# A gated DeltaNet trunk on one core: the causal mask moves from TensorE and the exponent to a clamp on ScalarE and a select on GpSimd

## The chip, the cores and the metric

The kernel runs on one core of a Trainium2 chip. The metric is the device time of one execution in microseconds (us), as the median over several runs. The engines are named as the profile names them: PE is TensorE (PEld its weight load), DVE is VectorE, ACT is ScalarE, POOL is GpSimd, and SP is SyncE, which here issues most DMAs. All arrays are float32.

## The reference

The reference is a decoder trunk of two layers over 512 tokens of width 1024: a gated DeltaNet mixer (16 value heads, 8 query and key heads, head dimension 128), a gated MLP with a short convolution, a sliding-window attention over shared keys and values, a second such MLP, and a final norm. The change lies in the mixer. Cut to what matters there (`gc` is the running sum of the log gates within a chunk, which only falls):

```python
diff = gc[..., :, None] - gc[..., None, :]
decay = jnp.where(tril, jnp.exp(jnp.where(tril, diff, 0.0)), 0.0)
m = jnp.where(strict, jnp.einsum('bnhcd,bnhsd->bnhcs', k_beta, k) * decay, 0.0)
t_mat = lax.linalg.triangular_solve(m + eye, eye, left_side=True, lower=True, unit_diagonal=True)
a_intra = jnp.einsum('bnhcd,bnhsd->bnhcs', q, k) * decay
def step(state, inp):
    w_i, u_i, qd_i, kd_i, a_i, gl_i = inp
    v_new = u_i - jnp.einsum('bhcd,bhde->bhce', w_i, state)
    o_i = (jnp.einsum('bhcd,bhde->bhce', qd_i, state)
           + jnp.einsum('bhcs,bhse->bhce', a_i, v_new))
    state = state * gl_i[..., None, None] + jnp.einsum('bhcd,bhce->bhde', kd_i, v_new)
```

So two matrices are needed per head and chunk: `m`, for the triangular solve, and `a_intra`, the attention weights within the chunk. Both are products of keys or queries with the same decay, and both are zero on one side of the diagonal.

## The kernel before

Everything is kept transposed: 128 channels on the partitions, 512 tokens along the free dimension, and chunks of 128 tokens. A dense product is a *pass* of 24 matmuls (L162, L163, L164 in `mm3`): eight blocks of 128 input channels, each as high half of the weights times high half of the input, high times low, and low times high. The halves of the weights come from a staged load: ACT casts a tile of 128x1024 to the high half `whi` (L132) and DVE subtracts to get the low half `wlo` (L133). There are three buffers of each, two stages, three PSUM banks `d` for the passes, and two banks `g` which the gate products share with the transposes.

The mixer's 16 heads are worked in four groups of four. Each group goes through jobs that are named by letters:

- K projects a key (conv and Silu, `conv_silu`, L277 to L281); B makes the products of the keys of a chunk with themselves (L433, copied out by ACT at L434) and the norms (a square root on ACT, L446).
- P (`key_products`, L458 to L486) makes the decay and the matrix for the solve. Per head a matmul (L464) spreads the running gates `gr` of that head over a bank of 128x512. A second matmul (L465), identity times a mask of 0 and -2^100, adds the mask to the same bank. Four Exp on ACT (L475), one per chunk of 128 tokens with the negated gate of the partition as bias, leave the decay in the row `dt`. DVE scales it (L477) and multiplies it with the key products (L479), and SP writes the diagonal blocks to DRAM for the solve.
- I solves the 32x32 blocks on DVE (L555, L561); L joins them to 128x128 (`levels`, short products on PE with copies by ACT: pz at L587 and L588, p6s at L608).
- Q projects and R normalises queries, A (`query_products`, L504 to L512) multiplies keys and queries (L508) and then the scaled decay (L511, DVE) into the tile `at`. T turns the keys, V projects values (scaled copies vt on ACT, L538).
- C is one step of the scan over the chunks: products with the state (L635), the solve's inverse (L651), a copy us by ACT (L653), products with the keys and with `at` (L659), squares on ACT (L682).
- z and g are the output gates (Silu sz on ACT, L705) and the gated norms of a finished group (L720 on ACT).

The table ORDER gives the jobs of each group in a row and the scheduler gives them priorities by their place, with an offset by letter (SHIFT); the dense passes of the jobs K, Q, V and z are thus spread between the short products. The order on each engine is then decided by a scheduler that simulates the program when it is built: it takes the ready instruction of highest priority, so an instruction that becomes ready later or lasts longer changes the order behind it. What has been put into an engine's row is executed in that order: an engine waits at the first instruction that is not ready. A function that ACT has not loaded needs an ACT_TABLE_LOAD ahead of it.

The job order of the first group, and the offsets:

```python
"K1 B P0 P1 I0 I1 V0 I2 I3 T1 Q0 Q1 A1 A0 V1 R T0 V2 V3 L0 L1 C0 C1 C2 C3",
...
SHIFT = {"R": 6, "B": -28, "g": -40, "K": -1, "N": 7, "C": -2, "P": -3}
```

The output gates and norms of one group run beside the next, and behind the mixer come the output projection, MLP, attention and MLP (from about 430 us on), which the change does not touch.

Of the kernel before, what the change touches and what calls it, by code (L numbers as in the profile page):

```python
# [8 lines left out]
F32 = mybir.dt.float32  # L9
F32R = mybir.dt.float32r  # L10
BF16 = mybir.dt.bfloat16
AF = mybir.ActivationFunctionType
ALU = mybir.AluOpType
# [4 lines left out]
P = 128  # L18
T = 512
NC = T // P  # L20
# [21 lines left out]
def kernel(  # L42
# [27 lines left out]
    V, S, G, PE, SP = nc.vector, nc.scalar, nc.gpsimd, nc.tensor, nc.sync  # L70
# [1 line left out]


    cp = ctx.enter_context(tc.tile_pool(name="const", bufs=1))
    cp.tile([P, 40], F32, name="gap_x")
    dp = ctx.enter_context(tc.tile_pool(name="scratch", bufs=1, space=DRAM))

    cnt = [0]
# [1 line left out]
    def nm(s):  # L80
        cnt[0] += 1
        return f"{s}_{cnt[0]}"
# [24 lines left out]
    def row(tag, dt=F32, n=T):  # L107
        return main.tile([P, n], dt, tag=tag, bufs=ROWS[tag], name=nm(tag))

    def pair(tag, dt=F32):  # L110
        return main.tile([P, 2, T], dt, tag=tag, bufs=PAIRS[tag], name=nm(tag))

    def bank(tag):
        return psum.tile([P, T], F32, tag=tag, bufs=BANKS[tag], name=nm(tag))

    def const(shape, dt=F32, s="c"):
        return cp.tile(list(shape), dt, name=nm(s))
# [64 lines left out]
    def together(makes, *after):  # L182
        first = None
        for make in makes:
            if first is None:
                first = make()
                for a in after:
                    behind(first, a)
            else:
                with tc.high_priority(JUMP):  # L190
                    behind(make(), first)
# [16 lines left out]
    for i in range(2):  # L208
        cs = slice(HQK * P + i * P, HQK * P + (i + 1) * P)
# [3 lines left out]

    ident = const([P, P], s="ident")
    make_identity(nc, ident[:])
    identr = const([P, P], F32R, s="identr")
    S.copy(identr[:], ident[:])
    ones = const([P, P], s="ones")
    V.memset(ones[:], 1.0)
    epsc = const([P, 1], s="eps")  # L220
# [42 lines left out]
    for k in range(KD):  # L263
        ps = bank("g") if k % 2 else bank("s")
        for c in range(NC):
            PE.transpose(ps[:, c * P : (c + 1) * P], xs[c][:, k * P : (k + 1) * P], ident[:])
        h, l = row("xh", F32R), row("xl", F32R)
# [65 lines left out]
    for c in range(NC):  # L333
        cs = slice(c * P, (c + 1) * P)
        V.tensor_tensor_scan(R[32:48, cs], ones[32:48, 0:P], sp_r[32:48, cs], 0.0, op0=ALU.mult, op1=ALU.add)
    for c in range(NC):
        cs = slice(c * P, (c + 1) * P)
# [4 lines left out]
    gr = row("gr", F32R)[:, :]  # L342
# [8 lines left out]
    G.affine_select(sk[:], sk[:], pattern=[[-1, 16]], compare_op=ALU.not_equal, fill=1.0, base=-32, channel_multiplier=1)  # L351
    skr = const([P, 16], F32R, s="skr")
    S.copy(skr[:], sk[:])
    mneg = row("acc", n=P)
    G.memset(mneg[:], 0.0)
    G.affine_select(
        mneg[:],
        mneg[:],
        pattern=[[1, P]],
        compare_op=ALU.is_ge,  # L360
        fill=-(2.0**100),
        base=0,
        channel_multiplier=-1,
    )
    mnegr = const([P, P], F32R, s="mnegr")
    S.copy(mnegr[:], mneg[:])

    gtp = bank("g")
    turned_gates = [
        PE.transpose(gtp[:, c * 80 : c * 80 + 80], R[0:80, c * P : (c + 1) * P], ident[0:80, 0:80])  # L370
# [5 lines left out]
    def hc(ap):  # L376
        return ap.rearrange("p c h -> p h c")

    beta_t, gc_t, gd_t = hc(gt[:, :, 0:16]), hc(gt[:, :, 32:48]), hc(gt[:, :, 64:80])
    ngc = const([P, 16, NC], s="ngc")  # L380
    V.tensor_scalar(ngc[:], gc_t, -1.0, None, op0=ALU.mult)
    egc = const([P, 16, NC], s="egc")
    S.activation(egc[:], gc_t, AF.Exp)
    negegc = const([P, 16, NC], s="negegc")
# [73 lines left out]
    def key_products(g, i):  # L458
        st[g]["nt", i] = pair("nt")
        for j in range(2):  # L460
            hh = 2 * i + j
            h = 4 * g + hh
            ps = bank("g")
            PE.matmul(ps[:], skr[:, h : h + 1].to_broadcast([P, P]), gr, start=True, stop=False)  # L464
            PE.matmul(  # L465
                ps[:].rearrange("p (c t) -> p c t", c=NC),
                identr[:],
                mnegr[:].unsqueeze(1).to_broadcast([P, NC, P]),
                start=False,
                stop=True,  # L470
            )
            dt = row("dt")
            for c in range(NC):
                cs = slice(c * P, (c + 1) * P)
                S.activation(dt[:, cs], ps[:, cs], AF.Exp, bias=ngc[:, h, c : c + 1])  # L475
            d3 = dt[:].rearrange("p (c t) -> p c t", c=NC)
            V.tensor_tensor(d3, d3, brk[:, h, :].unsqueeze(2).to_broadcast([P, NC, P]), op=ALU.mult)  # L477
            nt = st[g]["nt", i][:, j, :]
            V.tensor_tensor(nt, st[g]["kk"][:, i, :], dt[:], op=ALU.mult)  # L479
            for b in range(4):  # L480
                bs = slice(32 * b, 32 * b + 32)
                SP.dma_start(
                    nd[g, hh, :, b, :, :].rearrange("n s c -> s n c"),
                    nt[bs, :].rearrange("p (n c) -> p n c", n=NC)[:, :, bs],
                )
            st[g]["dt", hh] = dt  # L486
# [17 lines left out]
    def query_products(g, i):  # L504
        pq = bank("g")
        k, q = st[g]["k"][:, i, :], st[g]["q"][:, i, :]
        cut = [slice(c * P, (c + 1) * P) for c in range(NC)]
        together([lambda cs=cs: PE.matmul(pq[:, cs], k[:, cs], q[:, cs], start=True, stop=True) for cs in cut])  # L508
        at = pair("at")
        for j in range(2):  # L510
            V.tensor_tensor(at[:, j, :], pq[:], st[g]["dt", 2 * i + j][:], op=ALU.mult)  # L511
            st[g]["at", 2 * i + j] = at[:, j, :]  # L512

    def key_tokens(g, i):
# [220 lines left out]
    def bias_rows():  # L735
# [14 lines left out]
    JOBS = {  # L750
        "K": key_proj,
        "P": key_products,
        "I": solve,
        "Q": query_proj,
        "A": query_products,
        "T": key_tokens,
        "V": value_proj,
# [7 lines left out]
    base = tc.cur_priority  # L765
    pos = 0
    for i, line in enumerate(ORDER):
        for word in line.split():
            a, n = word[0], [int(d) for d in word[1:]]
# [77 lines left out]
    for m2 in range(KD // 2):  # L847
        sts = [load_stage(a_w_out[0], 1024 * u, 8, 256 * m2) for u in range(2)]
        for j in range(2):
            m = 2 * m2 + j  # L850
            ps = bank("d")
# [592 lines left out]
```

## Time and profile before

| | |
|---|---|
| median of 3 runs | 1417.68 us (1416.81 to 1419.02) |
| span of the profiled execution | 1412.6 us |
| PE, DVE, ACT, POOL busy | 1384.7, 1108.1, 748.1, 15.6 us |
| mean granted clock of PE, by stage | 1.00 throughout |
| gate products L464 and L465, first to last | 49.5 to 320 us |
| table loads on ACT | 36 |

The three runs' times are those of whole executions; the profiled one is known by its span, which lies 5.1 us under their median. "Busy" adds the time that an engine was executing; matmuls overlap, so the distance from start to start tells more of what one costs than its own length. An idle time is put down to the instruction that released the engine. In an answer of the trace `L132 ACT CAST whi<-stage 128x1024 ... x2` is line 132, engine, operation, the tile written and the tile read, shape, and how many such instructions were taken together.

### The profile page before, as it was taken

The page shows a single profiled execution, that of the slowest core. Times are in us where ns is not written, and L with a number is a line of the kernel's source. Part 1 is how long each engine was busy: PE and PEld are TensorE (multiplying, and loading weights), DVE is VectorE, ACT ScalarE, POOL GpSimd, SP SyncE. Part 2 cuts the span into 40 slices and gives each one's busy share as a digit, 9 for nine tenths or more (in the row PEclk, how much of TensorE's full clock was granted, in tenths as well). Part 3 has the DMA queues.
Part 4 walks back from the last instruction along what each step waited for, and adds up shares of the span by engine and source line. Part 5 has one row for each costly group of instructions (what it writes and reads, how often), then busy time and mean ns, then how long its engine had stood idle before and what let it go on. Part 6 is the DMA issues. An engine that isn't in the chain of part 4 may idle for free.

```text
span 1412.6 us, 21751 instructions
## 1 busy us (share of the span) xinstructions
PE 1384.7 (98%) x8370; PEld 1167.1 (83%) x8370; DVE 1108.1 (78%) x2070; ACT 748.1 (53%) x1470; POOL 15.6 (1%) x37
## 2 busy tenths in 40 slices
PE   7999999999999999999999999999999999999998
PEld 5787888878877888888988889777788888988897
DVE  4996896978856438879878889788668888878996
ACT  7764566656658225444344446567544444444543
POOL 1000000000100000000000000000000000000000
PEclk9999999999999999999999999999999999999999
DMA  5333254172465323221443223322132231432222
GB/s 161 92 103 115 79 175 126 61 231 84 140 225 159 119 90 112 90 90 46 135 150 119 75 79 109 109 71 76 61 112 90 90 101 49 146 106 82 92 75 75
DMA packets 162299, 151.80 MB, mean 107 GB/s; under 512 B 24148, under 2 KB 150677, under 8 KB 162197
## 3 DMA queue, kind: packets, MB, share of 16 engines
q1 hardware_dynamic: 159938, 150.22, 33.2%
q8 instruction: 66, 1.08, 0.3%
q10 hardware_dynamic: 2259, 0.20, 0.1%
q14 instruction: 36, 0.29, 0.1%
HBM read 133.60 MB, written 15.75 MB: 106 GB/s over the span
## 4 chain that ended last, share of the span: by engine, by line
PE 87%; DVE 6%; DMA 2%; ACT 2%; issue 1%; SPq 0%; DVEq 0%; ACTq 0%
PE d L162 20%; PE d L163 20%; PE d L164 20%; PE g L198 2%; DVE wlo L133 2%; PE d L1054 1%; PE d L1207 1%; PE d L1211 1%; PE d L1209 1%; PE d L1052 1%; PE d L1053 1%; PE s L1054 1%; PE s L1052 1%; PE s L1053 1%; PE s L659 1%
## 5 line engine op out<-in xcount | busy, mean ns | idle before, releaser
L162 PE MATMUL d<-xh,whi 128*128 128x512 f32 x1128 | 444.2, 394 | 0.2
L163 PE MATMUL d<-xl,whi 128*128 128x512 f32 x1128 | 444.0, 394 | 0.0
L164 PE MATMUL d<-xh,wlo 128*128 128x512 f32 x1128 | 441.9, 393 | 0.3 <-DVE wlo L156 0.3
L132 ACT CAST whi<-stage 128x1024 fp32r<-128x1024 f32 (+2 forms) x234 | 227.4, 976 | 247.7 <-PE d L163 165.1
L133 DVE TENSOR_TENSOR wlo<-stage,whi 128x1024 fp32r<-128x1024 f32 (+2 forms) x234 | 263.4, 1128 | 70.4 <-ACT whi L132 69.6
L162 PEld LDWEIGHTS d<-xh,whi 128*128 128x128 f32 x1128 | 211.7, 188 | 44.9 <-ACT xh L172 0.5
L164 PEld LDWEIGHTS d<-xh,wlo 128*128 128x128 f32 x1128 | 211.6, 188 | 44.6 <-DVE wlo L156 0.7
L163 PEld LDWEIGHTS d<-xl,whi 128*128 128x128 f32 x1128 | 211.7, 188 | 43.2 <-issue 0.5
L280 DVE SCALAR_TENSOR_TENSOR acc<-d,cwc,acc 128x511 f32<-128x511 f32 (+2 forms) x96 | 70.7, 739 | 8.7 <-ACT acc L277 7.9
L913 DVE TENSOR_TENSOR sz<-d,p6s 128x512 f32<-128x512 f32 x59 | 40.6, 688 | 42.9 <-PE d L164 40.7
L935 ACT ACTIVATE dt<-dt 128x512 f32<-128x512 f32 x44 | 27.8, 631 | 78.3 <-DVE dt L918 78.3
L918 DVE SCALAR_TENSOR_TENSOR dt<-sz,fcw,dt 128x511 f32<-128x511 f32 (+1 forms) x60 | 44.8, 747 | 1.8 <-ACT dt L916 0.9
L918 DVE SCALAR_TENSOR_TENSOR va<-sz,fcw,va 128x511 f32<-128x511 f32 (+1 forms) x58 | 43.3, 747 | 0.9
L561 DVE TENSOR_TENSOR sT<-sT,p6s 64x31 f32<-64x31 f32 (+15 forms) x124 | 40.9, 330 | 2.0
L555 DVE TENSOR_TENSOR p6s<-sN,sT 64x31 f32<-64x31 f32 (+15 forms) x124 | 40.7, 328 | 1.9
L1276 ACT ACTIVATE dt<-dt,sm 128x256 f32<-128x256 f32 (+1 forms) x64 | 30.1, 471 | 21.5 <-DVE sm L1259 21.5
L132 ACT CAST whi<-st 128x768 fp32r<-128x768 f32 (+1 forms) x30 | 23.7, 792 | 30.5 <-PE g L1053 9.0
L913 DVE TENSOR_TENSOR zl<-d,p6s 128x512 f32<-128x512 f32 x29 | 20.0, 688 | 17.8 <-PE d L164 17.8
L682 ACT ACTIVATE rq<-o 128x128 f32<-128x128 f32 x64 | 19.0, 301 | 25.4 <-DVE o L677 22.3
L937 DVE TENSOR_TENSOR va<-dt,va 128x512 f32<-128x512 f32 x44 | 30.4, 690 | 1.2
L133 DVE TENSOR_TENSOR wlo<-st,whi 128x768 fp32r<-128x768 f32 (+1 forms) x30 | 26.8, 899 | 2.2 <-ACT whi L132 2.2
L916 ACT ACTIVATE dt<-sz,normc,fcw 128x512 f32<-128x512 f32 x30 | 24.5, 815 | 6.5 <-DVE sz L913 6.0
(770 smaller groups left out, 2876.2 us busy)
## 6 DMA issues: line engine op xcount, KB each, us to landing
stage<-in_ffn_w_up_dram SPq DMA_DIRECT2D x44, 1024.0 KB, 4.8
stage<-in_a_w_in_dram SPq DMA_DIRECT2D x23, 1024.0 KB, 5.8
stage<-in_ffn_w_down_dram SPq DMA_DIRECT2D x16, 768.0 KB, 4.3
stage<-in_a_w_out_dram SPq DMA_DIRECT2D x8, 1024.0 KB, 5.0
st<-in_ffn_w_down_dram SPq DMA_DIRECT2D x8, 768.0 KB, 5.3
zd<-sz SPq DMA_DIRECT2D x16, 256.0 KB, 2.6
od<-o SPq DMA_DIRECT2D x16, 256.0 KB
stage<-in_b_w_q_dram SPq DMA_DIRECT2D x4, 1024.0 KB, 5.0
```

What stands on the lines that cost most here:

```text
L132: S.copy(hi[:, :kt, :m], src)
L133: V.tensor_tensor(lo[:, :kt, :m], src, hi[:, :kt, :m].bitcast(F32), op=ALU.subtract)
L162: PE.matmul(ps, hi[:, k, :m], xh[k], start=first and k == 0, stop=False)
L163: PE.matmul(ps, hi[:, k, :m], xl[k][:], start=False, stop=False)
L164: done.append(PE.matmul(ps, lo[:, k, :m], xh[k], start=False, stop=last and k == kt - 1))
L280: V.scalar_tensor_tensor(acc[:, d:], ps[:, : T - d], col, acc[:, d:], op0=ALU.mult, op1=ALU.add)
L555: V.tensor_tensor(tv, N[:, s, s + 1 : 32].unsqueeze(2).to_broadcast([64, n, m]), Tm[:, s : s + 1, 0:m].to_broadcast([64, n, m]), op=ALU.mult,)
L561: V.tensor_tensor(Tm[:, s + 1 : 32, 0:m], Tm[:, s + 1 : 32, 0:m], tv, op=ALU.subtract)
L913: V.tensor_tensor(u[:], ps[:], rs[:], op=ALU.mult)
L918: V.scalar_tensor_tensor(acc[:, d:], u[:, : T - d], tap(2 - d, t), acc[:, d:], op0=ALU.mult, op1=ALU.add)
L937: V.tensor_tensor(b[:], a[:], b[:], op=ALU.mult)
L1276: S.activation(ej, ej, AF.Exp, bias=ngm[:, i : i + 1], scale=-1.0, accum_out=den[:, i : i + 1])
```

## The change

The mask no longer enters before the Exp. L464 alone fills the bank with the gates along the free dimension. ACT takes from each chunk of 128 the clamped difference, Relu(gate of the partition minus gate along the row), with the gate itself as bias and a scale of -1, and then one Exp over the whole row of 128x512 with a scale of -1. On the causal side the clamp changes nothing (the running gates only fall); on the other side the decay is 1 where it was 0. The solve reads only one side of its blocks (L555 takes N above the diagonal, and `levels` takes the blocks on that side), while for the attention weights GpSimd writes zeros on the other side of `at`, with one affine_select of 128x512 per head behind L511. So per head one matmul of 128x512 and four Exp of 128x128 give way to four Relu of 128x128, an Exp of 128x512 and a select; the preparation of the mask, of the identity in the matmul's type and of the negated gates goes too. The pad `gap_x` grows from 40 to 104 columns.

```diff
-    identr = const([P, P], F32R, s="identr")
-    S.copy(identr[:], ident[:])
...
-    mneg = row("acc", n=P)
-    G.memset(mneg[:], 0.0)
...
-    mnegr = const([P, P], F32R, s="mnegr")
-    S.copy(mnegr[:], mneg[:])
...
-    ngc = const([P, 16, NC], s="ngc")
-    V.tensor_scalar(ngc[:], gc_t, -1.0, None, op0=ALU.mult)
...
-            PE.matmul(ps[:], skr[:, h : h + 1].to_broadcast([P, P]), gr, start=True, stop=False)
-            PE.matmul(
-                ps[:].rearrange("p (c t) -> p c t", c=NC),
-                identr[:],
-                mnegr[:].unsqueeze(1).to_broadcast([P, NC, P]),
-                start=False,
-                stop=True,
-            )
+            PE.matmul(ps[:], skr[:, h : h + 1].to_broadcast([P, P]), gr, start=True, stop=True)
             dt = row("dt")
             for c in range(NC):
                 cs = slice(c * P, (c + 1) * P)
-                S.activation(dt[:, cs], ps[:, cs], AF.Exp, bias=ngc[:, h, c : c + 1])
+                S.activation(dt[:, cs], ps[:, cs], AF.Relu, bias=gc_t[:, h, c : c + 1], scale=-1.0)
+            S.activation(dt[:], dt[:], AF.Exp, scale=-1.0)
...
             V.tensor_tensor(at[:, j, :], pq[:], st[g]["dt", 2 * i + j][:], op=ALU.mult)
+            a3 = at[:, j, :].rearrange("p (c t) -> p c t", c=NC)
+            G.affine_select(
+                a3, a3, pattern=[[0, NC], [1, P]], compare_op=ALU.is_ge, fill=0.0, base=0, channel_multiplier=-1
+            )
```

The scheduler makes a new order of it on every engine, from the gate products of group 0 to the last scan. In the changed kernel the lines stand some 18 to 20 earlier: L446 is the gate product, L450 the Relu, L451 the Exp, L275 and L279 the convolution and the Silu (L277 and L281 before), L428 the square root, L518 the scaled copies vt, L484 the products of keys and queries and L476 the squares of the queries, L685 the Silu of the output gates. L132 and L162 to L164 stay.

ACT in group 0, before. The cast at the top makes the high half of the weights of a value's pass (PE's bank d_797 here, d_790 in the changed kernel); the rows `dt` are the four heads' decays, `kT`, `qT`, `va`, `vt` keys, queries and values, `acc` the convolution:

```order
L132 CAST whi_798<-stage_795 128x1024
L475 ACTIVATE dt_449<-g_446,ngc_331 128x128 x4
L475 ACTIVATE dt_463<-g_460,ngc_331 128x128 x4
L446 ACT_TABLE_LOAD
L446 ACTIVATE nk_351<-sse_350 128x8
L475 ACT_TABLE_LOAD
L475 ACTIVATE dt_478<-g_475,ngc_331 128x128 x4
L475 ACTIVATE dt_492<-g_489,ngc_331 128x128 x4
L281 ACT_TABLE_LOAD
L281 ACTIVATE va_540<-acc_572 128x512
L281 ACTIVATE qT_631<-acc_663 128x512
L277 ACTIVATE acc_698<-d_669,cwc_204 128x512
```

ACT at the same place in the changed kernel, in two parts, between which four rows stand (a Relu of dt_466, the Exp of dt_451, three more Relu of dt_466 and the first of dt_480):

```order
L450 ACTIVATE dt_437<-g_435,gt_320 128x128 x4
L279 ACT_TABLE_LOAD
L279 ACTIVATE va_529<-acc_561 128x512
L428 ACT_TABLE_LOAD
L428 ACTIVATE nk_340<-sse_339 128x8
L451 ACT_TABLE_LOAD
L451 ACTIVATE dt_437<-dt_437 128x512
L450 ACTIVATE dt_451<-g_449,gt_320 128x128 x4
```

```order
L451 ACTIVATE dt_466<-dt_466 128x512
L450 ACTIVATE dt_480<-g_478,gt_320 128x128 x3
L518 ACTIVATE vt_567<-g_568,nk_340 128x128
L451 ACTIVATE dt_480<-dt_480 128x512
L518 ACTIVATE vt_567<-g_568,nk_340 128x128 x3
L279 ACT_TABLE_LOAD
L279 ACTIVATE qT_620<-acc_652 128x512
L275 ACTIVATE acc_687<-d_658,cwc_202 128x512
L275 ACTIVATE acc_743<-d_714,cwc_202 128x512
L132 CAST whi_791<-stage_788 128x1024
L132 CAST whi_837<-stage_788 128x1024
L132 CAST whi_1180<-stage_1177 128x1024
```

The cast of that value's weights has moved from ahead of the group's first Exp to behind its last, and two further casts follow it. PE at the same place in the changed kernel:

```order
L164 MATMUL d_714<-xh_194,wlo_716 128x512
L162 MATMUL d_790<-xh_131,whi_791 128x512
L163 MATMUL d_790<-xl_132,whi_791 128x512
L162 MATMUL d_836<-xh_131,whi_837 128x512
L163 MATMUL d_836<-xl_132,whi_837 128x512
L484 MATMUL g_693<-qT_620,kT_204 128x128 x4
L484 MATMUL g_703<-qT_620,kT_204 128x128 x4
L164 MATMUL d_790<-xh_131,wlo_792 128x512
```

The pass that writes d_790 follows at once on the pass of d_714, as it did before, but two products of the next pass and the products of keys and queries now stand between its own second and third product.

ACT in group 1 of the changed kernel, from the third head's Exp to the cast of the pass of d_1572 (pass 15, counting the passes of the mixer); before, the four heads' Exp stood in one block, a load and a Silu followed, and no sz stood ahead of that cast:

```order
L451 ACTIVATE dt_1312<-dt_1312 128x512
L450 ACTIVATE dt_1326<-g_1324,gt_320 128x128 x3
L279 ACT_TABLE_LOAD
L279 ACTIVATE qT_1410<-acc_1442 128x512
L451 ACT_TABLE_LOAD
L451 ACTIVATE dt_1326<-dt_1326 128x512
L275 ACTIVATE acc_1477<-d_1448,cwc_202 128x512
L685 ACT_TABLE_LOAD
L685 ACTIVATE sz_1535<-d_1506 128x512
L685 ACTIVATE sz_1567<-d_1538 128x512
L132 CAST whi_1573<-stage_1570 128x1024
```

What moved here is the last Exp, which now stands behind a Silu's load and takes a load of its own, and two Silu of output gates, which came ahead of the cast. Over the whole program ACT's order holds 41 table loads in place of 36; in group 2 and 3 the Relu and Exp are mixed with the copies p6s (L588 now) of the level products and with the copies us (L633 now) of the scan. From the first MLP on the order is the same.

More of the change, by code (lines that the diff above doesn't have):

```diff
@@ L74 @@
     cp = ctx.enter_context(tc.tile_pool(name="const", bufs=1))
-    cp.tile([P, 40], F32, name="gap_x")
+    cp.tile([P, 104], F32, name="gap_x")
     dp = ctx.enter_context(tc.tile_pool(name="scratch", bufs=1, space=DRAM))
@@ L353 @@
     S.copy(skr[:], sk[:])
-    mneg = row("acc", n=P)
-    G.memset(mneg[:], 0.0)
[L356 to L363, printed above, removed]
-    )
-    mnegr = const([P, P], F32R, s="mnegr")
-    S.copy(mnegr[:], mneg[:])
     gtp = bank("g")
@@ L463, in key_products @@
             ps = bank("g")
-            PE.matmul(ps[:], skr[:, h : h + 1].to_broadcast([P, P]), gr, start=True, stop=False)
-            PE.matmul(
-                ps[:].rearrange("p (c t) -> p c t", c=NC),
-                identr[:],
-                mnegr[:].unsqueeze(1).to_broadcast([P, NC, P]),
-                start=False,
-                stop=True,
-            )
+            PE.matmul(ps[:], skr[:, h : h + 1].to_broadcast([P, P]), gr, start=True, stop=True)
             dt = row("dt")
```

## Prediction

> **What bounds the kernel now.** I read the page first, then the busy time stage by stage, then who waits for whom, then single instructions around the places that the change touches. The page's span, its engine shares, the chain that ended last by engine, and one group of the dense products:
>
> ```profile
> span 1412.6 us, 21751 instructions
> PE 1384.7 (98%) x8370; PEld 1167.1 (83%) x8370; DVE 1108.1 (78%) x2070; ACT 748.1 (53%) x1470; POOL 15.6 (1%) x37
> PE 87%; DVE 6%; DMA 2%; ACT 2%; issue 1%; SPq 0%; DVEq 0%; ACTq 0%
> ```
>
> TensorE is busy for 98% of the span and carries 87% of the chain. The stages in which the change lies (columns: stretch, its length, then busy time and number of instructions of PE, PEld, DVE, ACT, POOL):
>
> ```profile
> 45.00:60.00 15.00, 14.37 (x71) 11.55 (x71) 14.19 (x31) 14.27 (x31) 0.00 (x0) 1.00 0.49 147
> 60.00:130.00 70.00, 69.96 (x339) 57.29 (x337) 59.66 (x124) 41.49 (x89) 0.00 (x0) 1.00 0.37 109
> 320.00:360.00 40.00, 40.00 (x343) 33.87 (x342) 36.28 (x92) 25.35 (x89) 2.45 (x8) 1.00 0.29 87
> ```
>
> PE hardly pauses. In the first stretch ACT has 0.7 us free in 15 us, since the mask and gate work of head group 0 falls into it. PE's waits from 45 to 430 us are four rows:
>
> ```profile
> PE g L235 <- DVE onwc L237: 1.7, 1, 1.7
> PE p L659 <- ACT us L653: 1.5, 1, 1.5
> PE g L198 <- ACT ol L720: 1.0, 1, 1.0
> PE d L162 <- ACT kT L168: 0.5, 1, 0.5
> ```
>
> So time that is taken from PE here would be gained, and every wait that the new order gives PE is lost in full: nothing behind it has slack to return it.
>
> **What is removed.** Sixteen matmuls of L465. Their group, and four PE instructions in order of time (start, duration):
>
> ```profile
> L465 PE MATMUL g<-mnegr,identr 128*128 128x512 f32 x16 | 6.3, 394 | 0.0
> 50.95 0.40 PE L464 MATMUL g<-gr,skr 128*128 128x512 f32 x1
> 51.18 0.39 PE L465 MATMUL g<-mnegr,identr 128*128 128x512 f32 x1
> 62.98 0.39 PE L162 MATMUL d<-xh,whi 128*128 128x512 f32 x1
> 63.21 0.39 PE L163 MATMUL d<-xl,whi 128*128 128x512 f32 x1
> ```
>
> A row lasts 0.39, but the next begins 0.23 later. The gain is 16 x 0.23 = 3.7 us, 0.92 per head group (by the rows' own length it would be 6.3; that overlaps, so I take 3.7). The dropped casts, the mask and the negated cumulative gates lie before 45 us, where PE does not wait for them: nothing.
>
> **What is added on ScalarE, group 0.** Its rows there (start, duration):
>
> ```profile
> 50.08 1.05 ACT L132 CAST whi<-stage 128x1024 fp32r<-128x1024 f32 x1
> 51.03 2.17 ACT L475 ACTIVATE dt<-g,ngc 128x128 f32<-128x128 f32 x8
> 53.23 1.28 ACT L446 ACT_TABLE_LOAD   x1
> 54.52 0.21 ACT L446 ACTIVATE nk<-sse 128x8 f32<-128x8 f32 x1
> 54.73 1.28 ACT L475 ACT_TABLE_LOAD   x1
> 59.52 0.63 ACT L281 ACTIVATE va<-acc 128x512 f32<-128x512 f32 x1
> 60.05 0.61 ACT L281 ACTIVATE qT<-acc 128x512 f32<-128x512 f32 x1
> 60.58 0.67 ACT L277 ACTIVATE acc<-d,cwc 128x512 f32<-128x512 f32 x1
> 61.15 1.14 ACT L538 ACTIVATE vt<-g,nk 128x128 f32<-128x128 f32 x4
> 62.15 1.07 ACT L132 CAST whi<-stage 128x1024 fp32r<-128x1024 f32 x1
> ```
>
> The cast at 50.08 makes the weights of the dense pass that PE starts at 62.98 (call it pass 7). It is ready at 51.13: 11.85 us of slack. In the changed order (shown with the change) it stands behind all of group 0's gate work. From these rows: 16 Relu at 2.17/8 = 0.27 make 4.3; four Exp over 128x512, by the 0.53 from one 128x512 activation to the next (59.52 to 60.05), 2.1; four table loads at 1.29 (53.23 to 54.52) 5.2; two Silu 1.06; the square root 0.21; the four scaled copies 1.0 (61.15 to 62.15); two L277 at 0.57 make 1.1. The sum is 15.0. From 50.08 that puts the cast at 65.1 and its end at 66.15. PE, four L465 earlier, gets to pass 7 at 62.98 - 0.92 = 62.06: it waits **4.1**. Then the order lets PE do two products of pass 7 and two of pass 8. Pass 8's weights come one cast later (0.95 after, 67.1), PE is there at 66.6: 0.5. The next products need a qT that ACT makes behind a third cast, at about 68.7; PE is there at 67.6: 1.1. Together 5.7 lost, 0.92 gained: **+4.8**. The Relu itself could cost anything between nothing and the Exp's price over the same shape; I take the latter, as both read the same bank and write the same row. The added Exp is bounded by 0.53 and the 0.63 that such a row lasts, which would make 0.4 more.
>
> [...]
>
> **Group 1.** ACT before, and the pass that PE starts with the first of the two casts (pass 15):
>
> ```profile
> 98.08 1.28 ACT L475 ACT_TABLE_LOAD   x1
> 106.58 1.28 ACT L281 ACT_TABLE_LOAD   x1
> 108.41 0.67 ACT L277 ACTIVATE acc<-d,cwc 128x512 f32<-128x512 f32 x1
> 108.98 1.99 ACT L132 CAST whi<-stage 128x1024 fp32r<-128x1024 f32 x2
> 110.87 0.59 ACT L705 ACTIVATE sz<-d 128x512 f32<-128x512 f32 x1
> 115.35 0.39 PE L162 MATMUL d<-xh,whi 128*128 128x512 f32 x1
> ```
>
> The cast ends at 110.0, 5.3 before its use. Ahead of it come four Exp (2.1), two more loads (2.6) and two Silu of L705 (some 0.55 each, 1.1): 5.8 later, so 115.8, and PE would be there at 114.43: 1.4. The second of those Silu reads the bank that pass 14 has just filled, so the cast cannot begin before that pass has ended: even if ACT has caught up, 0.55 + 1.05 = 1.6 behind it, less four short products that PE has there. So 1.4 to 1.6 for the cast itself; behind it pass 15 needs its low half and a qT, which cost 0.5 and 1.1 in group 0, and with some of that I take 2.6 (from 1.4 to 3.2), net **+1.7**.
>
> **Groups 2 and 3.** Here the products no longer stand in one block: in group 2 they are threaded through the level products and the first scan step of group 1, in group 3 through the scan of group 2. PE's short products there hang on ACT's copies. Two rows of before (the second a group with what it waited for):
>
> ```profile
> 231.09 0.76 ACT L608 COPY p6s<-p 64x256 f32<-64x256 f32 x2 [0.43 <-PE p L605]
> L653 ACT COPY us<-s 128x512 f32<-128x512 f32 x16 | 9.5, 594 | 11.2 <-PE s L651 11.1
> ```
>
> Today ACT stands ready for them (11.1 us idle for PE). Behind a load and an Exp (1.82) each copy comes up to 1.8 late, less the one to four dense products that PE has in between (0.23 each). For group 2 I count two such p6s copies at about 0.8, one us copy at 1.1, 0.5 for the bank that ACT has not emptied, and about 2.2 for the cast of pass 27, which now follows six loads and all Relu and Exp: 5.4. As these rest on the order alone I take 4.4, net **+3.5**. For group 3 five waits (us copies 0.7, 0.6 and 1.9, the last behind two loads, a Silu and an Exp; bank 0.9; state 0.4) are 4.5; about 1 us of the waits that before has there goes; with 0.92 gained, **+2.5**. Both could be as low as -0.9, if PE finds enough dense work, and as high as +6 and +5.
>
> **GpSimd.** Each of the 16 masks covers 128x512 on an engine that is 1% busy. Nearest rows:
>
> ```profile
> 2.03 0.52 POOL L343 MEMSET gr<- 128x512 f32 x1
> 19.20 0.55 DVE L133 TENSOR_TENSOR wlo<-gst,whi 128x384 fp32r<-128x384 f32 x1
> 19.29 0.61 POOL L356 TENSOR_SCALAR_AFFINE_SELECT acc<-acc 128x128 f32<-128x128 f32 x1
> masks.py:199 POOL TENSOR_SCALAR_AFFINE_SELECT ident<-ident 128x128 f32<-128x128 f32 x1 | 0.3, 292 | 0.0
> L511 DVE TENSOR_TENSOR at<-g,dt x4: 679/679/680, 67.7 to 69.5; 128x512 f32<-128x512 f32 x4
> L659 PE MATMUL s<-us,at x16: 275/275/275, 148.1 to 156.2; 128*128 128x128 f32 x16
> ```
>
> One costs between 0.5 (a memset of that size) and 4 x 0.61 = 2.4; I take 4 x 0.29 = 1.2, the same operation alone, 19 us in all. Group 0's masks follow L511 at 67.7 to 69.5 and the scan that reads them runs from 148.1: 78 us of cover, so they cost nothing. Behind them GpSimd has only memsets for later solves.
>
> **Sum.** 4.8 + 1.7 + 3.5 + 2.5 = +12.5. The profiled span of 1412.6 lies 5.1 under the median of 1417.68; I add to both alike: span 1425, time **1430**.
>
> **Rivals.**
> *Faster:* the gate work stays hidden and only 3.7 us go: 1414. It decides at group 0, if the ACT block ahead of pass 7's cast takes 11 us or less instead of 15.0, and if the threaded copies find PE busy. For it speak the slack of 11.85 and ACT's 53%; against it the sum of rows above, and that a first stretch with 0.7 us of free ACT time is given 3.4 more (four Exp and one load, 2.1 + 1.29). Chance 0.07.
> *Only the first two places bite:* in groups 2 and 3 PE's dense products cover the copies and only the gain remains there: 4.8 + 1.7 - 1.8 = +4.7, 1422, and down to 1418 if the Relu or the load is cheaper. The four rows of waits speak for it: today's interleaving works. Chance 0.15; a third of it within 0.2%.
> *GpSimd holds up VectorE:* the mask of 128x128 took 0.61 beside a DVE instruction and 0.29 without. If the two exclude each other, DVE stands still for 16 x 1.2 to 2.4 = 19 to 38 us, of which the free sixth to tenth of DVE in these stretches (59.66 of 70, 36.28 of 40) cannot hide all, and low weight halves come late: some +6 on top, 1436, up to 1440. Chance 0.10.
> [...]
> My forecast as worked out: 0.68.
>
> **Range and chances.** 1418 to 1440: from both later groups near -0.9, to their upper ends or the GpSimd case. A difference under 0.2% (2.8 us) is about what a measurement of this kernel can't tell from none. Faster 0.07; same 0.08 (the low end of the second rival, and a little of the forecast); slower 0.85.
>
> **What would show it.** In the changed profile: PE's waits list d L162 <- ACT whi of about 4 us near 62, one of 1 to 2 us near 115, and us or p6s copies among PE's releasers from 200 to 360; ACT has 41 table loads for 36; L465 is gone, 3.7 us less PE work. From 430 us on the order is unchanged and so must be the length. It would be wrong if PE's waits in 45 to 430 stay near 5 us, or if DVE waits for POOL or the masks' readers do.

## The result and the profile after

The changed kernel takes 1427.88 us (median of 4 runs, 1426.90 to 1428.38) where the kernel before takes 1417.24 (median of 4, 1416.39 to 1419.02): slower by 10.6 us, a ratio of 1.0075 with a 95% interval of 1.0055 to 1.0094. The forecast was 1430, in 1418 to 1440.

The page of the changed kernel, its span, its engine shares and the granted clock of PE in 40 slices (before, that row held nothing under 9):

```profile
span 1426.5 us, 21762 instructions
PE 1387.7 (97%) x8354; PEld 1168.6 (82%) x8354; DVE 1110.8 (78%) x2069; ACT 761.7 (53%) x1489; POOL 24.6 (2%) x51
...
PEclk9899999999999999999999999999999999999999
...
PE 84%; ACT 6%; DVE 6%; DMA 3%; issue 1%; SPq 0%; DVEq 0%; ACTq 0%
```

PE lost sixteen matmuls, and yet its busy time rose by 3.0 us: some of its work ran at a lower clock. ACT, 2% of the chain before, now holds 6%. Who PE waits for from 45 to 480 us (total, times, longest), the largest rows:

```profile
PE d L162 <- ACT whi L132: 6.3, 2, 4.1
PE g L233 <- DVE onwc L235: 1.7, 1, 1.7
PE p L639 <- ACT us L633: 1.6, 3, 0.7
PE s L592 <- ACT p6s L588: 1.0, 2, 0.5
PE s L572 <- ACT pz L568: 0.8, 1, 0.8
PE g L198 <- ACT va L279: 0.8, 1, 0.8
PE d L162 <- DVE acc L278: 0.8, 1, 0.8
```

Group 0 in the changed kernel: ACT from the first Relu on, then PE around the pass that the text calls pass 7:

```profile
51.23 1.14 ACT L450 ACTIVATE dt<-g,gt 128x128 f32<-128x128 f32 x4
52.39 1.28 ACT L279 ACT_TABLE_LOAD   x1
...
57.15 0.63 ACT L451 ACTIVATE dt<-dt 128x512 f32<-128x512 f32 x1
57.69 1.38 ACT L450 ACTIVATE dt<-g,gt 128x128 f32<-128x128 f32 x5
...
63.48 1.28 ACT L279 ACT_TABLE_LOAD   x1
64.77 0.63 ACT L279 ACTIVATE qT<-acc 128x512 f32<-128x512 f32 x1
...
66.45 2.93 ACT L132 CAST whi<-stage 128x1024 fp32r<-128x1024 f32 x3
```

```profile
63.07 0.40 PE L164 MATMUL d<-xh,wlo 128*128 128x512 f32 x1
67.54 0.79 PE L162 MATMUL d<-xh,whi 128*128 128x512 f32 x1 [4.08 <-ACT whi L132]
68.13 0.63 PE L163 MATMUL d<-xl,whi 128*128 128x512 f32 x1
69.53 0.77 PE L162 MATMUL d<-xh,whi 128*128 128x512 f32 x1 [0.77 <-DVE acc L278]
```

From the first Relu to the cast ACT works 15.2 us, and PE waits 4.08. The rows behind the wait last 0.6 to 0.8 where such a row lasted 0.39. The busy time by stage tells why (the third column from the end is the granted clock):

```profile
64.00:68.00 4.00, 0.46 (x1) 0.46 (x2) 3.28 (x7) 3.99 (x6) 0.00 (x0) 0.77 0.23 36
68.00:72.00 4.00, 3.23 (x11) 2.30 (x11) 4.00 (x6) 2.64 (x4) 0.00 (x0) 0.50 0.25 67
72.00:76.00 4.00, 4.00 (x25) 3.58 (x24) 3.96 (x11) 0.05 (x1) 2.51 (x4) 0.88 0.59 170
...
420.00:424.00 4.00, 3.04 (x36) 2.56 (x36) 3.76 (x6) 3.14 (x6) 0.30 (x1) 0.64 0.51 143
424.00:428.00 4.00, 4.00 (x15) 3.30 (x14) 2.69 (x5) 0.00 (x0) 0.00 (x0) 0.50 0.59 184
```

The clock fell to half within the pause of PE, at 66.2, and stayed there for 6.8 us; it fell again at 421.1, behind the waits from 416 us on, for another 6.8.

To see where the time went I compare the start of the same dense product in two traces, counted by the dense products (24 to a pass). A lag that grows is time lost in that stretch, as long as the same products of other jobs stand ahead of both marks. Up to pass 34 that holds but for the removed products and eight transposes. At pass 48 the changed kernel still has 78 level products of group 3 ahead of it. At pass 54 only the sixteen removed products differ.

| dense pass | before, us | after, us | lag | in that stretch |
|---|---|---|---|---|
| 10 | 83.72 | 91.47 | +7.8 | +7.8, group 0 |
| 24 | 194.34 | 205.19 | +10.8 | +3.1, group 1 and the start of group 2 |
| 34 | 281.76 | 294.93 | +13.2 | +2.3, group 2 |
| 48 | 399.52 | 407.83 | +8.3 | -4.9, 78 level products of group 3 put off |
| 56 | 473.53 | 488.68 | +15.2 | +6.8, the last group's scan and the first products behind it |
| end (span) | 1412.6 | 1426.5 | +13.9 | -1.2, the rest |

The whole stretch from 45 us to the start of pass 54 tells what the lag is made of, before and after (length, then PE's busy time):

```profile
45.00:462.65 417.65, 413.74 (x2912) 338.16 (x2912) 330.08 (x702) 262.20 (x676) 9.60 (x20) 1.00 0.44 136
```

```profile
45.00:477.80 432.80, 418.05 (x2896) 340.01 (x2896) 331.26 (x699) 275.73 (x697) 19.36 (x36) 0.98 0.43 130
```

PE stood idle for 3.9 us before and for 14.8 after, 10.8 more. It was also busy for 4.3 us longer, although 3.7 us of products are gone: some 7 to 8 us of the 15.2 are products that ran at half clock (at 45.7 to 49.1, 66.2 to 73.0 and 421.1 to 428.0), not waits.

The difference of the two spans is 13.9, that of the medians 10.6. The profiled execution of before was a short one: over the runs of this study whose span and time are both known, the time lies 1.7 to 2.1 above the span, so it took some 1414.3 to 1414.7, between 2.5 and 3 under its median.

### The profile page after: what moved, and what is told of

The parts are those of the page before. It is cut to its first block, busy times and chain, and to the rows that moved or that the text cites. A ratio compares the mean times of both kernels' runs of the same rounds, so it can differ in the third digit from the quotient of the medians.

```text
span 1426.5 us, 21762 instructions
## 1 busy us (share of the span) xinstructions
PE 1387.7 (97%) x8354; PEld 1168.6 (82%) x8354; DVE 1110.8 (78%) x2069; ACT 761.7 (53%) x1489; POOL 24.6 (2%) x51
## 4 chain that ended last, share of the span: by engine, by line
PE 84%; ACT 6%; DVE 6%; DMA 3%; issue 1%; SPq 0%; DVEq 0%; ACTq 0%
PE d L162 19%; PE d L164 19%; PE d L163 19%; PE g L198 2%; DVE wlo L133 1%; PE d L1034 1%; PE d L1187 1%; PE d L1191 1%; PE d L1189 1%; PE d L1032 1%; PE d L1033 1%; PE s L1034 1%; PE s L1032 1%; PE s L631 1%; PE s L1033 1%
## 5 line engine op out<-in xcount | busy, mean ns | idle before, releaser
L162 PE MATMUL d<-xh,whi 128*128 128x512 f32 x1128 | 444.1, 395 | 7.4 <-ACT whi L132 6.3
L164 PE MATMUL d<-xh,wlo 128*128 128x512 f32 x1128 | 442.4, 394 | 0.9 <-DVE wlo L133 0.5
L132 ACT CAST whi<-stage 128x1024 fp32r<-128x1024 f32 (+2 forms) x234 | 226.9, 975 | 239.6 <-PE d L163 150.9
L162 PEld LDWEIGHTS d<-xh,whi 128*128 128x128 f32 x1128 | 211.8, 188 | 53.6 <-ACT whi L132 9.5
L164 PEld LDWEIGHTS d<-xh,wlo 128*128 128x128 f32 x1128 | 211.4, 188 | 45.0 <-DVE wlo L133 1.0
L278 DVE SCALAR_TENSOR_TENSOR acc<-d,cwc,acc 128x511 f32<-128x511 f32 (+2 forms) x96 | 70.6, 739 | 4.7 <-ACT acc L275 4.0
L132 ACT CAST whi<-st 128x768 fp32r<-128x768 f32 (+1 forms) x30 | 23.7, 791 | 29.7 <-PE p L1033 5.8
```

What stands on the lines that cost most here:

```text
L132: S.copy(hi[:, :kt, :m], src)
L162: PE.matmul(ps, hi[:, k, :m], xh[k], start=first and k == 0, stop=False)
L164: done.append(PE.matmul(ps, lo[:, k, :m], xh[k], start=False, stop=last and k == kt - 1))
L278: V.scalar_tensor_tensor(acc[:, d:], ps[:, : T - d], col, acc[:, d:], op0=ALU.mult, op1=ALU.add)
```

## The experiments

Each was timed in three rounds, beside the kernel before on the same chip (its medians there: 1416.85 beside the first four kernels below, 1416.49 beside the two with the cast first, the late group and the late cast, 1416.42 beside the early group and the clamps on VectorE, 1415.48 beside the last order).

**The selects alone, both ways.** Do GpSimd's masks hold anything up?

```diff
 changed kernel:
-            G.affine_select(
-                a3, a3, pattern=[[0, NC], [1, P]], compare_op=ALU.is_ge, fill=0.0, base=0, channel_multiplier=-1
-            )
 kernel before:
+            G.affine_select(
+                a3, a3, pattern=[[0, NC], [1, P]], compare_op=ALU.is_ge, fill=0.0, base=0, channel_multiplier=-1
+            )
```

> The changed kernel without the sixteen GpSimd selects; the weights of the scan keep a decay of 1 on the far side of the diagonal, so this part of the computation is left out. ACT's and PE's orders are row for row those of the changed kernel. If the time went to waits for ScalarE and to the clock behind them: 1426 to 1429 us, the same waits. If GpSimd holds up VectorE: at least 3 us less than the changed kernel, 1424 or lower.

> The kernel before with the sixteen selects added behind the masked products, which changes no value; ACT's and PE's orders are those of before. ScalarE theory: 1416 to 1418.5 us, as before. GpSimd theory: 1420 or more.

Without the selects: 1427.69 (1.0078, 1.0063 to 1.0093). With them in the kernel before: 1417.49 (0.9995, 0.9983 to 1.0007). The selects cost nothing that can be measured; the rival with GpSimd falls. Their group in the changed kernel, with the mean of one (in ns) and what GpSimd waited for:

```profile
L489 POOL TENSOR_SCALAR_AFFINE_SELECT at<-at 128x512 f32<-128x512 f32 x16 | 12.8, 799 | 138.9 <-DVE at L487 138.7
```

The second of these runs shows something else. Its PE and ACT have the very order of the kernel before, and the two traces run within 0.9 us of each other up to pass 48. Then its profile loses 4.6 us. The same stretch in the kernel with the selects, and in the kernel before:

```profile
424.00:428.00 4.00, 1.22 (x9) 1.03 (x8) 0.68 (x3) 1.58 (x5) 0.00 (x0) 1.00 0.78 290
428.00:432.00 4.00, 3.77 (x17) 3.52 (x18) 1.52 (x3) 2.40 (x5) 0.00 (x0) 0.57 0.45 126
```

```profile
424.00:428.00 4.00, 3.67 (x24) 3.29 (x25) 2.93 (x7) 2.62 (x5) 0.00 (x0) 1.00 0.45 151
428.00:432.00 4.00, 4.00 (x24) 3.39 (x22) 3.11 (x8) 3.41 (x14) 0.00 (x0) 1.00 0.48 175
```

One pause of 3.0 us, for a gated row that ACT splits late (kT, L168), and a half clock behind it: with one order of PE and ACT the tail of the mixer can differ by that much between two executions. This kernel's ten runs spread from 1413.35 to 1419.14; that the spread comes from the tail is not shown.

**The clamp alone, mask products kept.**

```diff
 kernel before:
-                S.activation(dt[:, cs], ps[:, cs], AF.Exp, bias=ngc[:, h, c : c + 1])
+                S.activation(dt[:, cs], ps[:, cs], AF.Relu, bias=gc_t[:, h, c : c + 1], scale=-1.0)
+            S.activation(dt[:], dt[:], AF.Exp, scale=-1.0)
```

> The kernel before with its mask products kept, but with four Relu and one Exp of 128x512 per head in place of four Exp; 39 table loads. The scheduler leaves the cast of pass 7 ahead of the gate work here. If the order of that cast decides: place 1 is hidden, the later groups cost some us, 1419 to 1424. If the longer chain on ScalarE costs its time wherever the casts stand: as the changed kernel plus the 3.7 us of the mask products, 1430 to 1433. If ScalarE is not the cause: 1416 to 1419.

1432.08 us (1.0110, 1.0095 to 1.0126): the changed kernel's time and 4.2 more, as the second reading had it. So the clamp on ScalarE, with the mask products kept, is enough for more than the whole loss, and not through the cast of pass 7, which is hidden here: the lag at pass 8 is +0.7, then +5.2 at pass 10 (a wait of 2.2 us for a convolution, and half clock), +6.0 at pass 48, and +17.2 at pass 56. Some two thirds of it arise in the tail. From 45 us to pass 54 PE is idle 7.8 us more than before, and busy 9.4 us longer with the same products: the clock was at half from 416.9 to 430.6.

**The removal without the clamp.**

```diff
 changed kernel:
-                S.activation(dt[:, cs], ps[:, cs], AF.Relu, bias=gc_t[:, h, c : c + 1], scale=-1.0)
-            S.activation(dt[:], dt[:], AF.Exp, scale=-1.0)
+                S.activation(dt[:, cs], ps[:, cs], AF.Exp, bias=ngc[:, h, c : c + 1], scale=0.05)
...
+    V.tensor_scalar(ngc[:], gc_t, -0.05, None, op0=ALU.mult)
```

> The mask products go and GpSimd selects, but there is no clamp: four Exp per head as before, with 0.05 times the differences so that the far side stays finite; the decays are thus other numbers. 37 table loads. The scheduler puts the cast of pass 7 behind the gate work here too, since without the mask product the Exp are ready earlier. If cast order and ScalarE's time both count: without the four long Exp of group 0 (2.1 us) the cast ends near 64.0 where PE comes at 62.06, so a wait of about 2 us and no fall of the clock; 1415 to 1420. If any new order costs what the changed kernel's does: 1425 or more. If only the clamp's instructions cost: 1412 to 1414.5.

1420.32 us (1.0025, 1.0015 to 1.0035). ScalarE does what it did before, with one table load more, and PE less, and still nothing is gained: the two parts of the change do not add up, since each makes a new order. PE's longest wait, and the stage behind it with its clock:

```profile
PE d L162 <- ACT whi L132: 2.1, 1, 2.1
```

```profile
68.00:72.00 4.00, 4.00 (x18) 3.84 (x18) 2.28 (x4) 0.42 (x1) 1.12 (x2) 0.50 0.10 35
```

The wait is the 2.1 that was worked out, from the cast's place alone; but the clock did fall behind it, which I had not expected after so short a pause. The lag is +6.4 at pass 10 (part of it from a half clock at 45.5 to 48.9, ahead of the cast), falls to +1.7 by pass 48, where level products of group 3 are put off as in the changed kernel, and is +7.9 at pass 56.

**The cast first, with and without the clamp.** An order of issue is added, so that the gate work of group 0 stands behind the cast of pass 7, once in the changed kernel, once in the one with plain Exp:

```diff
+    behind(relus[0, 0], pass_cast[2304])
...
 with plain Exp:
+    behind(gates[0, 0], pass_cast[2304])
```

> The changed kernel with one order of issue added: the first Relu of head 0 stands behind the cast of pass 7. In the profile of the changed kernel PE waited 4.1 us for that cast and lost 7.8 by pass 8 to 10. If that cast's place is what costs: 1419 to 1422 us. If the longer ScalarE work of each group costs wherever the casts stand, as the kernel with mask and clamp says: 1425 to 1428.

> No mask product, GpSimd selects, four plain Exp with 0.05 times the differences (other decays), and the cast of pass 7 ahead of the gate work as before. ScalarE has the work of before, PE 3.7 us less. If the removal is worth its PE time once nothing is put in its way: 1411 to 1414 us. If the new order alone costs, in the last group too: 1416 to 1420.

With the clamp 1423.89 (1.0062, 1.0038 to 1.0085), between the two readings. Each against its own measurement of before, this kernel costs 7.4 us and the changed kernel 10.6, so the cast's place is worth some 3 us, and as the intervals overlap not even that is sure. The new order has 44 table loads, and PE now waits 3.1 us in the same place for a convolution on DVE (L280). Without the clamp 1419.45 (1.0023, 1.0006 to 1.0040). There little is in PE's way up to pass 34: twelve products, 2.8 us, are gone by then, and it is 1.2 us ahead of before, with a half clock at 45.9 to 49.3 against it. At pass 56 it is 5.5 behind. From 45 us to pass 54 PE is idle for 7.1 us, where before had 3.9, and the clock is at half a second time, from 411.2 to 418.0. So the 3.7 us of PE work are gained at first and lost again in the tail.

**The last group alone, late.**

```diff
 kernel before, in key_products:
+            g0 = PE.matmul(ps[:], skr[:, h : h + 1].to_broadcast([P, P]), gr, start=True, stop=False)
+            if h == 12:
+                behind(g0, steps[2, 1][0])
...
```

> The kernel before, with the gate products of group 3 held back behind the second scan step of group 2; the first 255 rows of ACT are those of before. No engine gets more work. The decays of group 3 come some 15 to 20 us later, about as late as in the changed kernel. If the solve, the level products and the scan of the last group set the end of the mixer: 1421 to 1426 us, with PE's waits behind 400 us. If only PE's waits in the earlier places count: 1415 to 1418.

1432.15 us (1.0115, 1.0100 to 1.0130), 6 more than the upper end that I gave. No engine does more, nothing up to pass 36 moves (lag -0.2), and 16 us are lost. The last multiplication of group 3's decays with the key products (`nt`), in before, in the changed kernel and here, and the square root of its norms in the same three (the first row holds two multiplications; the last begins at 326.6):

```profile
326.03 1.29 DVE L479 TENSOR_TENSOR nt<-m,dt 128x512 f32<-128x512 f32 x2
...
437.42 0.22 ACT L698 ACTIVATE fc<-fc 128x16 f32<-128x16 f32 x1
```

```profile
344.59 0.69 DVE L455 TENSOR_TENSOR nt<-m,dt 128x512 f32<-128x512 f32 x1
...
454.65 0.22 ACT L678 ACTIVATE fc<-fc 128x16 f32<-128x16 f32 x1
```

```profile
353.93 0.68 DVE L481 TENSOR_TENSOR nt<-m,dt 128x512 f32<-128x512 f32 x1
...
456.68 0.21 ACT L705 ACTIVATE fc<-fc 128x16 f32<-128x16 f32 x1
```

Between the two stand a solve of some 44 us on DVE (336.9 to 380.8 before), the level products and four scan steps, each waiting for the one before. It is seen by following one group through the engines, not by looking at one engine. The group is 27 us late here, and 18 in the changed kernel, so the two are not the same delay.

Most of the 16 us are not waits. The stretch from 45 us to the start of pass 54, and what follows a wait of 2.7 us for the solve's result from DRAM (to 410.4):

```profile
45.00:479.08 434.08, 425.63 (x2912) 344.81 (x2912) 328.65 (x700) 261.68 (x675) 6.54 (x20) 0.97 0.42 129
410.00:430.50 20.50, 18.20 (x243) 13.95 (x244) 9.88 (x17) 5.53 (x13) 0.61 (x2) 0.50 0.54 181
```

With the products of before PE is idle 4.5 us more and busy 11.9 us longer: the clock stood at half for 20.5 us, although PE was busy for 18.2 of them. What a late group costs is for the larger part this clock.

With plain Exp and the cast first, the last `nt` begins at 327.7, 1.1 late, but the last step of the solve at 387.4 (before 380.8) and the norms at 444.6: there the solve itself is held up on DVE.

**The late cast alone.** Nine copies of 128x128 on ACT behind the Exp of group 0, and the cast of pass 7 behind them, in the kernel before:

```diff
+            if h == 3:
+                for _ in range(9):
+                    fill.append(S.copy(padj[:], ident[:]))
+                behind(fill[0], gates[3, 3])
...
+    behind(pass_cast[2304], fill[-1])
```

> The kernel before, mask products kept, with nine copies of 128x128 put on ACT behind the Exp of group 0 and the cast of pass 7 behind them: the same late cast as in the changed kernel (end near 66.3), and nothing more in the other groups. Each wait lost in full: a hole of 3.4 us, about 1 us of waits behind it, and 2 us of half clock: 1422 to 1425 us. If later stages make up for it: 1417 to 1420.

1423.70 us (1.0054, 1.0039 to 1.0069): a wait of 3.10 and one of 0.65 behind it, half clock at 67.3 to 70.7, a lag of +5.0 at pass 10 and +8.3 at pass 56. What PE loses in group 0 is not returned by later stages. The 3.3 us that come on top cannot be put down to the cast: the later order is not that of before either (by pass 48 PE has 66 level products more behind it).

**The last group earlier, and more dense work beside it.** If a late last group costs so much, the changed kernel should gain by bringing it forward, or by keeping dense passes for its scan.

```diff
 changed kernel, the first:
-            target = base + 1000 * (100 + pos + SHIFT.get(a, 0))
+            target = base + 1000 * (100 + pos + SHIFT.get(a, 0) - (12 if i == 3 and a in "KBPI" else 0))
 changed kernel, the second:
-    "K0 K1 B n P0 P1 I0 I1 I2 z I3 Q0 Q1 R A1 z z A0 T0 V0 V1 V2 T1 V3 L0 L1 g g g g C0 C1 C2 C3 N",
-    "z g z z z g g g",
+    "K0 K1 B n P0 P1 I0 I1 I2 I3 Q0 Q1 R A1 A0 T0 V0 V1 V2 T1 V3 L0 L1 g C0 C1 C2 C3 N",
+    "z z z z g g g g z z z g g g",
```

> The changed kernel with the key, norm, gate and solve jobs of group 3 twelve places earlier in the priorities; all instructions are those of the changed kernel, and groups 0 to 2 keep their order. In the new order the Relu and Exp of group 3 stand between the first and the second us copy of the scan of group 2. If the last group's chain sets the end of the mixer: some 5 us less than the changed kernel, 1420 to 1424, though PE waits as much in groups 0 to 2. If only PE's own lost time counts: 1426 to 1429.

> The changed kernel with the job order of its last two rows altered: three output-gate passes and three gated norms of the last but one group go behind the last group's scan jobs, so that one and a half dense passes more are left to run beside that scan (its products stand at passes 48 to 49 in place of 49.4 to 50.4). Groups 0 to 2 keep their work. If the last 7 us of the changed kernel's loss come from the last scan having too few dense products beside it: 1420 to 1424 us. If, as with the jobs of group 3 moved earlier, the output projection then waits for other rows: 1427 or more.

1429.79 us (1.0086, 1.0060 to 1.0111) and 1441.33 (1.0181, 1.0150 to 1.0212). Both miss. The first brings group 3's norms to 441.6, 13 us earlier than in the changed kernel (in an execution 4.7 us above its median), and gains nothing. PE then waits for the rows that enter the output projection; the first row of each one's waits:

```profile
PE d L162 <- ACT kT L168: 7.5, 3, 6.5
```

```profile
PE d L162 <- ACT kT L168: 7.4, 3, 6.3
```

ACT's split in turn waited for a row from DRAM (4.8 and 4.7 us, `yd`). So the last group's chain is not alone at the end: the gated rows of the other heads, which come over DRAM and are split by ACT, stand close behind it, and in these two orders they take its place.

**The clamp on VectorE.** Two versions that compute what the changed kernel does, with the clamp off ScalarE:

```diff
 the first:
-                S.activation(dt[:, cs], ps[:, cs], AF.Relu, bias=gc_t[:, h, c : c + 1], scale=-1.0)
-            S.activation(dt[:], dt[:], AF.Exp, scale=-1.0)
+                V.tensor_scalar(dt[:, cs], ps[:, cs], gc_t[:, h, c : c + 1], 0.0, op0=ALU.subtract, op1=ALU.min)
+            S.activation(dt[:], dt[:], AF.Exp)
 the second, in place of the same Relu and Exp:
+            V.tensor_tensor(
+                dt[:].rearrange("p (c t) -> p c t", c=NC),
+                ps[:].rearrange("p (c t) -> p c t", c=NC),
+                gc_t[:, h, :].unsqueeze(2).to_broadcast([P, NC, P]),
+                op=ALU.min,
+            )
...
+                S.activation(dt[:, cs], dt[:, cs], AF.Exp, bias=ngc[:, h, c : c + 1])
```

> The clamp goes from ScalarE to VectorE (four subtract-and-min of 128x128 per head out of PSUM), one Exp of 128x512 stays on ScalarE; selects and the missing mask product as in the changed kernel. ScalarE then has 0.55 us per head less than before, VectorE some 1 us more; 38 table loads, the cast of pass 7 stands first. If ScalarE's chain is what costs: PE waits in groups 0 and 1 go, 1415 to 1420. If the last group's chain, which passes through VectorE, takes it over: 1420 to 1425.

> The clamp as one minimum of 128x512 per head on VectorE (gates along the row against the gate of the partition), then four Exp on ScalarE as in the kernel before; no mask product, selects on GpSimd. ScalarE as before with 35 loads, VectorE 0.7 us more per head, the cast of pass 7 first. ScalarE theory: 1414 to 1418 us. Last group's chain: 1418 to 1422.

1434.12 us (1.0116, 1.0092 to 1.0140) and 1424.17 (1.0054, 1.0034 to 1.0073). In the first the convolutions of group 0 come late on DVE, and PE waits for them and for ACT:

```profile
PE d L162 <- DVE acc L278: 4.2, 1, 4.2
PE d L162 <- ACT sz L685: 2.8, 1, 2.8
```

In the second PE is level with before or ahead of it up to pass 48 (+0.2 at pass 34), has no wait over 1.7, and ends the mixer 9.6 late: the last `nt` of group 3 begins at 328.6, the last step of its solve at 388.9, its norms at 449.8. Its clock was at half from 406.0 to 423.1. VectorE is on the last group's chain, and the solve ends 8.1 us later than before where `nt` was 2.0 later; that the added minimums make the solve late is argued, not shown. None of the versions that were tried beats the kernel before.

## Why the prediction was right, point by point

**Group 0: right in mechanism, 3.0 us too small.** The block ahead of the cast was put at 15.0 and took 15.2; the wait at 4.1 and was 4.08, with both of its ends some 1.4 later than forecast. Pass 8's wait was put at 0.5 and was 0.77, but for another reason: it ended with the convolution on DVE (acc, L278), not with the second cast. An ACT_TABLE_LOAD at 63.48 is followed by its activation at 64.77, so the row's 1.29 was the price to take. What the sum lacked is the clock, which it put at nothing. Behind the wait PE ran at half clock to 73.0, some 4.7 us of it busy, 2.4 lost. Before the wait there is another fall:

```profile
45.34 0.49 PE L233 MATMUL g<-ident,f 128*128 128x128 f32 x2 [1.67 <-DVE onwc L235]
...
46.05 0.63 PE L164 MATMUL d<-xh,wlo 128*128 128x512 f32 x1
46.48 0.63 PE L162 MATMUL d<-xh,whi 128*128 128x512 f32 x1
```

That pause is the same in the kernel before (1.68) and cost its clock nothing; here products come 0.43 apart for 3.4 us, 1.7 lost. The kernel without the selects, with the same order, shows no such fall there and is 1.6 to 2.0 us ahead from then on. All 14 profiles have this pause, of 1.5 to 1.9 us, and six show a fall behind it. So this part is put down to chance rather than to the change. The third term, the qT that was to cost 1.1, cost nothing: at half clock PE came to it late enough.

**Group 1: right.** The cast behind two Silu cost a wait of 2.23 for the high half, inside the 1.4 to 3.2 that I gave to that pass; the stretch to pass 24 lost 3.1 net where 1.7 was forecast, with two more short waits in it (0.8 and 0.5).

**Groups 2 and 3: the sum about right, the mechanism not.** I forecast +3.5 and +2.5 by waits of PE for copies, banks and a cast; measured are +2.3 to pass 34 and +2.0 from there to pass 54. PE's idle time from pass 24 to 54 is 5.7 us (3.2 before) against some 9.9 counted. The copies (L639, L592, L572 in the rows above) are 3.4 of it, 2.7 of that behind 400 us, and for the cast of pass 27, counted at 2.2, PE did not wait at all. The step that failed is that each delay of a copy is paid by PE on the spot. PE had dense products to go on with, and the delay travelled on: group 3's last gate product comes 13.5 us later, with everything ahead of it, and its solve, levels and scan end 17 us later. In place of the missing waits stands the half clock at 421.1 to 428.0, some 3 us. The run with only those gate products late shows that a late group alone can cost 16 us, most of it at half clock, though it was later there; the two that brought the group forward show that it is not the only thing that ends there. Of the 6.8 us behind pass 48, 2.0 are more idle time and some 3 the half clock, and the rest goes with the level products that were put off. Which of these waits come from the last group's chain and which from the rows for the output projection stays open.

**The 3.7 us of the removed products.** Their price per product was right (0.23 from start to start), their worth was not: "time that is taken from PE here would be gained" fails in the tail. The kernel with plain Exp and the cast first is ahead by 1.2 at pass 34 and 5.5 behind at the end of the mixer, by more idle time and half clock there.

**GpSimd.** Taken at nothing, and it was nothing that could be measured; a select took 0.63 to 0.85 us (one 1.72) rather than 1.2.

**From 430 us on** order and length were forecast to stay. That holds only from pass 54 on (462.7 us before), where the length is the same but for 1.2 us. In the output projection ahead of it the products come in another order, and the lag grows from +10.4 at pass 50 to +15.2.

**The sum** of 12.5 is made of 16.2 us of waits less 3.7. Up to pass 54 the runs showed 10.8 us of waits and some 7 to 8 at half clock, less the same 3.7. So that the sum came out is in part luck: the waits were too many, and the clock was not in it. It was also added to the median as if the profiled execution were a typical one. Against that execution the change costs 13.9; against the median 10.6, because the profiled one was some 2.5 to 3 us short of it.

## What to carry to other kernels

When a kernel's engine order is made by a scheduler, read the change in that order first: an instruction that is ready earlier can pass a cast that another engine needs, and four activations can cost more than the matmul that they replace (here four Relu took 1.14 us of ACT, the matmul 0.23 of PE). Where PE is 98% busy, ask nevertheless which dependent chain ends last when the dense work runs out; what shortened PE's work gained nothing here in the end, and what delayed the last group was paid for the larger part (16 us for 27). A pause of PE can have a price beyond its length (here 4.08 us of pause and 2.4 lost behind it at a clock of 0.50): look at the granted clock of each stretch beside the waits, or PE looks busy where it is slow.

## What the runs showed of the hardware that was not expected

PE's granted clock fell to 0.50 in or behind pauses of 4.08, of 2.1 and of 1.67 us, and not behind the same pause of 1.68 in the kernel before, nor behind one of 2.23 at 123 us in the changed kernel. In the mixer it was measured there for 3.4 and twice for 6.8 us in the changed kernel, for 13.7 with mask and clamp and for 20.5 with the late group, and there PE was busy for 18.2 of the 20.5. A 128x512 product then starts 0.43 us after the last in place of 0.23. A select of 128x512 on GpSimd took 0.76 us (median of sixteen) where one of 128x128 took 0.29 (another, in the kernel before, 0.61), and sixteen of them moved the time by nothing that could be measured (0.9995).
